# Bank sums, load queue and transposes of a streamed fp32 block: eight small changes of order in one kernel

## The chip, the cores and the metric

One Trainium2 chip, one core. The metric is the device time of one execution in microseconds (us); the time before is the median of three runs. Engines: PE is TensorE (matmuls and transposes), ACT is ScalarE, DVE is VectorE, POOL is GpSimd, SP issues the loads. Each engine works through its own list of instructions in a fixed order, and waits for the others by semaphores.

## The reference

One layer with S = 256 tokens, width D = 2048 and a hidden width FF = 5632, all in float32:

```
h = x + W_out [ DiffAttn ; ConformerConv ]( RMSNorm(x) )
hn = rms_norm(h, norm2_g)
a  = hn @ w_gate ;  bu = hn @ w_up
y  = h + (silu(a) * bu) @ w_down
```

The input projection w_in has 5120 columns; attention and convolution work on its output, and w_out (2048 x 2048) joins them. The weights are about 200 MB, each read once. The second line to the last are the feed-forward network (FFN), whose eleven blocks of 512 hidden columns take most of the time.

## The kernel before

**Products and chunks.** A float32 product is made of three products of rounded operands: hi times hi, lo times hi and hi times lo, where hi is the operand rounded to PE's fast format and lo the rest. A chunk of weights is two k-tiles (128 x 1024 elements, 512 KB). SP loads it (L300) into one of four buffers `raw`, ACT rounds it to `whi` (L305), DVE subtracts to get `wlo` (L314), and PE runs 8 matmuls with `whi` (L344, L345) and then 4 with `wlo` (L350). Matmuls are 128 x 128 by 512 columns; the two halves of the tokens (m = 0, 1) are the output rows. `run_chunks` (L372) writes out all engines' work in the order of the chunks: a chunk's load and rounding stand two or three chunks (AHEAD, HI_AHEAD) ahead of its matmuls, its subtraction two (LO_AHEAD). All other work sits in generators; `resume()` takes each running one a step on, between the halves of a chunk and at its end. So a `yield` more or less in a generator moves that step by half a chunk in every engine's list. There is no reordering after that.

**The stages.** Input projection with the convolution as side work, up to about 240 us; attention; w_out, about 260 to 350 us; block 0 of the FFN, a plain gate and up product, 350 to 420; blocks 1 to 10; and the w_down products in three groups (FGROUPS: after blocks 3, 7 and 10).

**w_out and h.** `out_done` (L726) adds a 512-column part to `h` on DVE (L729). For each of its four k-tiles PE transposes h into one PSUM bank `ps_h` (L738), ACT writes the rounded, scaled tile `hhi` from the bank (L219), DVE the rest `hlo` from the same bank (L220), and ACT reads the bank a second time for an unrounded copy `hn` (L743), which the fast blocks need. Then ACT sums squares (L405).

**make_forms** (L802) multiplies hn by the rows' factor rstd2, spread over partitions by a matmul of a matrix of ones, which POOL fills (L805), with a diagonal (L813, `ps_r`), and makes the seven sums of hn's quarters, `fhi` and `flo`, in block 0.

**Fast blocks 1 to 10.** A block is a list of twelve units. An `s` unit takes a k-tile of each half of the weights' rows, gate and up together, in seven products of sums (21 matmuls, L898 to L900), which go to seven PSUM banks; DVE makes the sums `wt` (L873 to L875) and the lower halves `wl` (L881, L882) of the weights. `g` and `u` units are plain chunks of w_gate and w_up (12 matmuls, L915, L916, L921) for the remaining k-tiles in pairs (TWOS); they use `whi` and `wlo` as above, and go on in banks Q2 and Q4 (g) or Q3 and QX (u). The order of kinds is ORDER = "sggsggsuusuu", FIRST for block 1. A block uses all eight banks, so the next block's s unit needs them back: Q3 last, for the seventh product of its first unit. `products_done` (L956) adds banks once the last s unit is through; `block_done` (L974) starts after the last unit, adds Q3 and QX (L980), multiplies with the silu (L983), and after some steps `transposed` (L782) turns the result in two sets of four transposes (L789, `ps_a`), each rounded on ACT and split on DVE (L793).

**w_down.** `down_done` (L987) adds to `h` (L995) and, in the last group, stores to the output from SP's queue (L997), in which the loads of the weights stand too. Every third chunk of w_down loads into `spare_raw`, one of two large buffers of the pool `early` (tag wb), which the s units use else.

Of the kernel before, what the change touches and what calls it, by code (L numbers as in the profile page):

```python
# [12 lines left out]
F32 = mybir.dt.float32  # L13
# [5 lines left out]
P = 128  # L19
# [51 lines left out]
NS = 4  # L71
REST = [k for k in range(KD) if k % HK >= NS]
TWOS = [tuple(REST[i : i + 2]) for i in range(0, len(REST), 2)]
BY_DMA = []

ORDER = "sggsggsuusuu"

FIRST = "guggsusgssuu"

Q1, Q6, Q7, Q5, Q2, Q4, Q3, QX = range(8)  # L80

# [16 lines left out]
def tile_block(  # L98
# [273 lines left out]
    def run_chunks():  # L372
        n = len(chunks)
        i = j = 0
        for t in range(n):
            hi_lead, lo_lead = lead(t)
            while j < min(i, t + 1 + lo_lead):
                chunks[j]["split"](chunks[j])
                j += 1
            while i < min(n, t + 1 + hi_lead):  # L380
                if i in before:
                    before[i]()
                chunks[i]["load"](chunks[i])
                chunks[i]["round"](chunks[i])
                i += 1
                if hi_lead == lo_lead:
                    chunks[j]["split"](chunks[j])
                    j += 1
            while j < min(n, t + 1 + lo_lead):
                chunks[j]["split"](chunks[j])  # L390
                j += 1
            chunks[t]["multiply"](chunks[t])
            if chunks[t].get("spare_raw") is not None and chunks[t]["done"]:
                resume()
        while running:
            resume()
# [329 lines left out]
    def out_done(n, ps):  # L726
        cs = slice(n * N, (n + 1) * N)
        for m in range(NM):
            dve.tensor_tensor(h[m][:, cs], h[m][:, cs], ps[m], ALU.add)  # L729
        if n == 2:  # L730
            held[0] -= NM
        yield
        for t in range(N // P):
            k = n * (N // P) + t
            yield from room(1)
            pt = aux_ps.tile([P, N], F32, tag="aux", name="ps_h")
            for m in range(NM):
                pe.transpose(pt[:, m * P : (m + 1) * P], h[m][:, k * P : (k + 1) * P], ident)  # L738
            hT[k] = lhs_pair("h", k)
            split_scaled(hT[k], pt[:, :S], col("g2", k))  # L740
            if k % HK == 0:
                hn.append(early.tile([P, HK, S], F32, tag="wb", name="hn"))
            act.activation(hn[k // HK][:, k % HK, :], pt[:, :S], AF.Copy, scale=col("g2", k))  # L743
            if t % 2:
                yield
        for m in range(NM):
            square_sum(h[m][:, cs], ss2[m][:, n : n + 1])
        if n == D // N - 1:
            yield
            for m in range(NM):  # L750
                ss = small.tile([P, 1], F32, tag="ssh", name="ssh")
                dve.tensor_reduce(ss, ss2[m], AX.X, ALU.add)
                rsqrt_mean(rstd2[m], ss, D, EPS)
            yield
            yield
            prestack.close()
            ffn["pool"] = ctx.enter_context(tc.tile_pool(name="ffn", bufs=1))
            start(make_forms())
# [42 lines left out]

    def make_forms():  # L802
        fp = ffn["pool"]
        ones = fp.tile([P, P], F32, tag="sum0", name="ones")
        pool.memset(ones, 1.0)  # L805
        diag = fp.tile([P, S], F32, tag="sum1", name="diag")
        for m in range(NM):
            act.activation(diag[:, m * P : (m + 1) * P], ident, AF.Copy, scale=rstd2[m])
        yield
        yield  # L810
        ps = aux_ps.tile([P, N], F32, tag="aux", name="ps_r")
        for m in range(NM):
            pe.matmul(ps[:, m * P : (m + 1) * P], ones, diag[:, m * P : (m + 1) * P], start=True, stop=True)  # L813
        yield
        rb = fp.tile([P, S], F32, tag="sum2", name="rb")
        act.copy(rb, ps[:, :S])
        yield
        for i in range(2):
            for k in range(0, HK, 4):
                t = hn[i][:, k : k + 4, :]  # L820
                dve.tensor_tensor(t, t, rb.unsqueeze(1).to_broadcast([P, 4, S]), ALU.mult)
                yield

        nr = HK - NS
        chi = fp.tile([P, 2 * nr, S], F32R, tag="chi", name="chi")
# [101 lines left out]
    def fast_block(j, order, after_down):  # L927
# [20 lines left out]
            users = [c for c in units if q in c["uses"]]  # L948
            users[0]["first"][q] = users[-1]["last"][q] = True
        [c for c in units if c["kind"] == "s"][-1]["done"] = products_done  # L950
        units[-1]["done"] = lambda sums: block_done(j, sums)
        chunks.extend(units)

    halfway = {}
# [1 line left out]
    def products_done(q):  # L956

        fp = ffn["pool"]
        w1, u2, u3, w4 = (fp.tile([P, N], F32, tag=f"sum{i}", name=f"sum{i}") for i in range(4))
        act.copy(w1, q[Q1])  # L960
        yield
        yield
        dve.tensor_tensor(u2, q[Q6], w1, ALU.add)
        dve.tensor_tensor(u3, q[Q7], u2, ALU.add)
        dve.tensor_tensor(w4, q[Q5], u3, ALU.add)
        dve.tensor_tensor(u2, q[Q5], u2, ALU.add)
        yield
        dve.tensor_tensor(w1, q[Q2], w1, ALU.add)
        dve.tensor_tensor(u3, q[Q4], u3, ALU.add)
        act.activation(w1, w1, AF.Silu)  # L970
        act.activation(u3, u3, AF.Silu)
        halfway.update(g=(w1, u3), u=(u2, w4))

    def block_done(j, q):  # L974
        while "g" not in halfway:
            yield
        g, u = halfway.pop("g"), halfway.pop("u")
        yield
        for m, i in enumerate((Q3, QX)):
            dve.tensor_tensor(u[m], q[i], u[m], ALU.add)  # L980
        yield
        for m in range(NM):
            dve.tensor_tensor(u[m], u[m], g[m], ALU.mult)  # L983
        yield from lag(3)
        yield from transposed(j, u)

    def down_done(g, n, ps):  # L987
        cs = slice(n * N, (n + 1) * N)
        parts = 2 if g == len(FGROUPS) - 1 and n == D // N - 1 else 1
        for m in range(NM):  # L990
            for i in range(parts):
# [2 lines left out]
                hs = slice(cs.start + i * w, cs.start + (i + 1) * w)  # L994
                dve.tensor_tensor(h[m][:, hs], h[m][:, hs], ps[m][:, ws], ALU.add)  # L995
                if g == len(FGROUPS) - 1:
                    sp.dma_start(out=out[m * P : (m + 1) * P, hs], in_=h[m][:, hs])  # L997
        yield


# [13 lines left out]
    for ks, first, last in ((range(0, 4), True, False), (range(4, 8), False, False), (range(8, 16), False, True)):  # L1014
        for n in range(3):
            block(w_out, n * N, ks, fm, (lambda ps, n=n: out_done(n, ps)) if last else None,
                  bkey=("o", n), first=first, last=last, spare=n == 2)
    block(w_out, 3 * N, range(16), fm, lambda ps: out_done(3, ps))
    j0 = 0
    for g, nb in enumerate(FGROUPS):  # L1020
        for j in range(j0, j0 + nb):
# [6 lines left out]
        for n in range(D // N):  # L1028
            at = len(chunks)
            block(w_down, n * N, range(j0 * 4, (j0 + nb) * 4), fa, lambda ps, g=g, n=n: down_done(g, n, ps))  # L1030
            for i, c in enumerate(chunks[at:]):
                c["spare_raw"] = i % 3 == 2
        j0 += nb

# [31 lines left out]
```

## Time and profile before

| what | value |
|---|---|
| runs of the kernel before | 1108.98, 1111.71, 1112.03 us (median 1111.71) |
| the profiled execution's own time | 1109.13 us |
| its span on the core (first to last instruction) | 1107.3 us |
| around the span | 1.83 us |
| mean of matmuls 128 x 128 by 512, start to start, when nothing waits | 0.23 us |

The profile is one execution. In a row of the timeline stand start, busy time, engine, line, operation, output and inputs, their shape, how many (x2), and in brackets the engine's idle time just before and what ended it. A row "PE q L898 <- DVE sum L980: 8.8, 7, 3.2" of the waits says that PE's line 898 waited for DVE's line 980, 8.8 us in total, 7 times, 3.2 us at most. The busy time of a matmul is from its start to its modelled end; matmuls overlap, so the distance of starts is what a matmul costs.

### The profile page before, as it was taken

The page shows a single profiled execution, that of the slowest core. Times are in us where ns is not written, and L with a number is a line of the kernel's source. Part 1 is how long each engine was busy: PE and PEld are TensorE (multiplying, and loading weights), DVE is VectorE, ACT ScalarE, POOL GpSimd, SP SyncE. Part 2 cuts the span into 40 slices and gives each one's busy share as a digit, 9 for nine tenths or more (in the row PEclk, how much of TensorE's full clock was granted, in tenths as well). Part 3 has the DMA queues.
Part 4 walks back from the last instruction along what each step waited for, and adds up shares of the span by engine and source line. Part 5 has one row for each costly group of instructions (what it writes and reads, how often), then busy time and mean ns, then how long its engine had stood idle before and what let it go on. Part 6 is the DMA issues. An engine that isn't in the chain of part 4 may idle for free.

```text
span 1107.3 us, 13190 instructions
## 1 busy us (share of the span) xinstructions
PE 1064.9 (96%) x4836; PEld 869.4 (79%) x4836; DVE 867.2 (78%) x1051; ACT 574.2 (52%) x755; POOL 43.6 (4%) x78
## 2 busy tenths in 40 slices
PE   8999999999999998799999999999999999999988
PEld 7888888877867776587888887777788888777766
DVE  4799899898745678999664599999965589998643
ACT  6544566756755555555343455555543355554332
POOL 0030111201000000000000000000000000000000
PEclk9999999999999999999999999999999999999999
DMA  8756655544544455665445765656446666545173
GB/s 238 218 182 193 196 168 172 162 158 149 176 151 172 152 175 206 207 214 167 152 170 192 247 226 161 224 182 196 151 151 214 208 224 232 179 162 185 63 246 115
DMA packets 118734, 203.02 MB, mean 183 GB/s; under 512 B 6932, under 2 KB 28878, under 8 KB 118668
## 3 DMA queue, kind: packets, MB, share of 16 engines
q1 hardware_dynamic: 118608, 202.14, 55.3%
q8 instruction: 38, 0.62, 0.2%
q14 instruction: 28, 0.23, 0.1%
q10 hardware_dynamic: 60, 0.03, 0.0%
HBM read 200.04 MB, written 2.10 MB: 183 GB/s over the span
## 4 chain that ended last, share of the span: by engine, by line
PE 50%; DVE 9%; issue 2%; DMA 2%; ACT 1%; SPq 0%; DVEq 0%; ACTq 0%
PE acc L344 7%; PE acc L345 7%; PE acc L350 7%; PE q L916 5%; PE q L915 5%; PE q L921 5%; PE q L900 4%; PE q L898 4%; PE q L899 4%; DVE wlo L314 2%; DVE wl L882 1%; DVE wt L873 1%; DVE wl L881 1%; DMA wb<-in_w_gate_dram 1%; DMA raw<-in_w_down_dram 1%
## 5 line engine op out<-in xcount | busy, mean ns | idle before, releaser
L314 DVE TENSOR_TENSOR wlo<-raw,whi 128x1024 fp32r<-128x1024 f32 (+1 forms) x297 | 359.5, 1219 | 180.1 <-ACT whi L305 179.4
L305 ACT CAST whi<-raw 128x1024 fp32r<-128x1024 f32 (+1 forms) x297 | 309.2, 1048 | 249.5 <-PE acc L345 135.1
L344 PE MATMUL acc<-whi,ahi 128*128 128x512 f32 x384 | 150.6, 392 | 4.5 <-ACT whi L305 4.5
L345 PE MATMUL acc<-whi,alo 128*128 128x512 f32 x384 | 149.7, 390 | 0.2 <-DVE alo L793 0.2
L344 PE MATMUL acc<-whi,xhi 128*128 128x512 f32 (+1 forms) x352 | 130.9, 378 | 3.7 <-ACT xhi L219 3.0
L877 ACT CAST wh<-wt 128x2048 fp32r<-128x2048 f32 x40 | 76.5, 1913 | 106.2 <-DVE wt L875 106.2
L345 PE MATMUL acc<-whi,xlo 128*128 128x512 f32 (+1 forms) x352 | 129.4, 374 | 0.4 <-DVE xlo L220 0.4
L915 PE MATMUL q<-whi,chi 128*128 128x512 f32 x320 | 127.0, 397 | 0.0
L916 PE MATMUL q<-whi,clo 128*128 128x512 f32 x320 | 126.3, 395 | 0.0
L898 PE MATMUL q<-wh,fhi 128*128 128x512 f32 x280 | 111.6, 398 | 10.0 <-DVE sum L980 8.8
L900 PE MATMUL q<-wl,fhi 128*128 128x512 f32 x280 | 110.3, 394 | 4.5 <-DVE wl L882 3.7
L899 PE MATMUL q<-wh,flo 128*128 128x512 f32 x280 | 109.1, 390 | 0.0
L481 DVE SCALAR_TENSOR_TENSOR y<-upad,cw,y 128x256 f32<-128x256 f32 x240 | 103.5, 482 | 2.4 <-ACT y L474 1.9
L350 PE MATMUL acc<-wlo,ahi 128*128 128x512 f32 x384 | 103.0, 389 | 0.0
L882 DVE TENSOR_TENSOR wl<-wt,wh 128x2048 fp32r<-128x2048 f32 x40 | 91.5, 2289 | 7.2 <-ACT wh L877 7.2
L350 PE MATMUL acc<-wlo,xhi 128*128 128x512 f32 (+1 forms) x352 | 88.2, 375 | 1.2 <-DVE wlo L314 1.2
L344 PEld LDWEIGHTS acc<-whi,ahi 128*128 128x128 f32 x384 | 72.1, 188 | 20.4 <-ACT whi L305 5.8
L921 PE MATMUL q<-wlo,chi 128*128 128x512 f32 x320 | 86.9, 393 | 0.0
L345 PEld LDWEIGHTS acc<-whi,alo 128*128 128x128 f32 x384 | 72.1, 188 | 15.7 <-DVE alo L793 1.0
L350 PEld LDWEIGHTS acc<-wlo,ahi 128*128 128x128 f32 x384 | 72.0, 188 | 15.0
L344 PEld LDWEIGHTS acc<-whi,xhi 128*128 128x128 f32 x352 | 67.3, 191 | 15.4 <-ACT xhi L219 3.4
L345 PEld LDWEIGHTS acc<-whi,xlo 128*128 128x128 f32 x352 | 67.3, 191 | 11.9 <-DVE xlo L220 0.9
(192 smaller groups left out, 1384.3 us busy)
## 6 DMA issues: line engine op xcount, KB each, us to landing
raw<-in_w_down_dram SPq DMA_DIRECT2D x88, 512.0 KB, 4.0
raw<-in_w_in_dram SPq DMA_DIRECT2D x48, 512.0 KB, 3.5
raw<-in_w_gate_dram SPq DMA_DIRECT2D x48, 512.0 KB, 4.4
raw<-in_w_up_dram SPq DMA_DIRECT2D x48, 512.0 KB, 3.7
wb<-in_w_up_dram SPq DMA_DIRECT2D x40, 512.0 KB, 3.6
wb<-in_w_gate_dram SPq DMA_DIRECT2D x40, 512.0 KB, 4.5
raw<-in_w_out_dram SPq DMA_DIRECT2D x32, 512.0 KB, 3.5
raw<-in_w_in_dram SPq DMA_DIRECT2D x62, 256.0 KB, 3.2
```

Of the source, the lines that this page charges most:

```text
L305: act.copy(c["hi"], c["raw"])
L314: dve.tensor_tensor(c["lo"], c["raw"], c["hi"].bitcast(F32), ALU.subtract)
L344: pe.matmul(ps[m], xhi[:, ms], hi[:, j, :], start=c["first"] and j == 0, stop=False)
L345: pe.matmul(ps[m], xlo[:, ms], hi[:, j, :], start=False, stop=False)
L350: pe.matmul(ps[m], xhi[:, ms], lo[:, j, :], start=False, stop=c["last"] and j == nk - 1)
L481: dve.scalar_tensor_tensor(y[:, ct, :], src, wk, y[:, ct, :], ALU.mult, ALU.add)
L898: pe.matmul(ps, fhi[:, f, p, :], c["hi"][:, w], start=bool(first), stop=False)
L899: pe.matmul(ps, flo[:, f, p, :], c["hi"][:, w], start=False, stop=False)
L900: pe.matmul(ps, fhi[:, f, p, :], c["lo"][:, w], start=False, stop=bool(last))
L915: pe.matmul(ps, x1[:, ms], hi[:, i, :], start=i == 0 and bool(c["first"].get(q)), stop=False)
L916: pe.matmul(ps, x2[:, ms], hi[:, i, :], start=False, stop=False)
L921: pe.matmul(sum_bank(c, q), forms["plain"][k][0][:, ms], lo[:, i, :], start=False, stop=i == 1 and bool(c["last"].get(q)))
```

## The change

Line numbers of the kernel after are one to seven lines off those before: `out_done` L744 to L747, products of s units L900 to L902, of g and u units L917, L918 and L923, DVE's wt L875 to L877 and wl L883, L884, the transposes L794 with their split L798, stores L998. L314, L980 and L983 are the same.

1. **By DMA.** The last residue pair of each block's g and u units (k-tiles 14 and 15) gets `wlo` in another way: ACT writes minus the rounded weights into it (L308), and a DMA issued by POOL (L309) adds `raw` to that. DVE's L314 is gone for these 20 chunks. POOL issued no DMA before.
2. **FIRST** is another order of kinds for block 1.
3. **prompt.** A block's or a w_down block's generator is stepped once more right after its last chunk; before, this was done for chunks whose key `spare_raw` was set at all.
4. **h.** `out_done` transposes two k-tiles into one bank, ACT reads the bank twice for `hn` (L744), rounds both tiles at once from `hn` in SBUF (L746), and DVE makes the rest from there (L747).
5. **make_forms** spreads the factor by an ACT write (`rep`) and two transposes, without POOL's ones, and has one step less.
6. **Bank sums.** A yield fewer or at another place in `products_done` and `block_done`; `lag(2)` for `lag(3)`.
7. **Stores** of the last w_down group go to POOL's queue, but for the last column part.
8. **Buffers.** Every third chunk of w_in and w_out, too, may load into `early`.

```diff
-BY_DMA = []
+BY_DMA = TWOS[-1:]
-FIRST = "guggsusgssuu"
+FIRST = "gugusgsgsusu"
...
-            if chunks[t].get("spare_raw") is not None and chunks[t]["done"]:
+            if chunks[t].get("prompt") and chunks[t]["done"]:
                 resume()
...
-        for t in range(N // P):
+        for t in range(0, N // P, 2):
             k = n * (N // P) + t
             yield from room(1)
-            pt = aux_ps.tile([P, N], F32, tag="aux", name="ps_h")
-            for m in range(NM):
-                pe.transpose(pt[:, m * P : (m + 1) * P], h[m][:, k * P : (k + 1) * P], ident)
-            hT[k] = lhs_pair("h", k)
-            split_scaled(hT[k], pt[:, :S], col("g2", k))
+            pt = aux_ps.tile([P, 2, S], F32, tag="aux", name="ps_h")
+            for i in range(2):
+                for m in range(NM):
+                    pe.transpose(pt[:, i, m * P : (m + 1) * P], h[m][:, (k + i) * P : (k + i + 1) * P], ident)
...
-            act.activation(hn[k // HK][:, k % HK, :], pt[:, :S], AF.Copy, scale=col("g2", k))
-            if t % 2:
-                yield
+            rows = hn[k // HK][:, k % HK : k % HK + 2, :]
+            for i in range(2):
+                act.activation(rows[:, i, :], pt[:, i, :], AF.Copy, scale=col("g2", k + i))
+            hi, lo = lhs_two("h", k)
+            act.copy(hi, rows)
+            dve.tensor_tensor(lo, rows, hi.bitcast(F32), ALU.subtract)
...
+            yield
...
-        ones = fp.tile([P, P], F32, tag="sum0", name="ones")
-        pool.memset(ones, 1.0)
-        diag = fp.tile([P, S], F32, tag="sum1", name="diag")
-        for m in range(NM):
-            act.activation(diag[:, m * P : (m + 1) * P], ident, AF.Copy, scale=rstd2[m])
-        yield
+        rep = fp.tile([P, S], F32, tag="sum1", name="rep")
+        for m in range(NM):
+            act.activation(rep[:, m * P : (m + 1) * P], ident, AF.Identity, bias=rstd2[m], scale=0.0)
...
-            pe.matmul(ps[:, m * P : (m + 1) * P], ones, diag[:, m * P : (m + 1) * P], start=True, stop=True)
+            pe.transpose(ps[:, m * P : (m + 1) * P], rep[:, m * P : (m + 1) * P], ident)
...
-        units[-1]["done"] = lambda sums: block_done(j, sums)
+        units[-1].update(done=lambda sums: block_done(j, sums), prompt=True)
...
         act.copy(w1, q[Q1])
         yield
-        yield
         dve.tensor_tensor(u2, q[Q6], w1, ALU.add)
         dve.tensor_tensor(u3, q[Q7], u2, ALU.add)
+        yield
         dve.tensor_tensor(w4, q[Q5], u3, ALU.add)
         dve.tensor_tensor(u2, q[Q5], u2, ALU.add)
-        yield
         dve.tensor_tensor(w1, q[Q2], w1, ALU.add)
+        act.activation(w1, w1, AF.Silu)
...
     def block_done(j, q):
...
         g, u = halfway.pop("g"), halfway.pop("u")
-        yield
         for m, i in enumerate((Q3, QX)):
             dve.tensor_tensor(u[m], q[i], u[m], ALU.add)
         yield
...
-        yield from lag(3)
+        yield from lag(2)
...
-                    sp.dma_start(out=out[m * P : (m + 1) * P, hs], in_=h[m][:, hs])
+                    (sp if n == D // N - 1 else pool).dma_start(out=out[m * P : (m + 1) * P, hs], in_=h[m][:, hs])
...
+    for i, c in enumerate(chunks[len(XPARTS) : -12]):
+        c["spare_raw"] = i % 3 == 2
```

The rounding and the accumulating DMA, which the kernel before has already but does not use since its BY_DMA is empty:

```
act.activation(c["lo"], c["raw"], AF.Copy, scale=-1.0)
pool.dma_start(out=c["lo"], in_=c["raw"].bitcast(F32R), accum_op=ALU.add)
```

**ACT at the first h transposes of w_out.** `hhi` and `hn` are the outputs for h (a pair of k-tiles has one `hhi`), `whi` the rounded weights, `junk` the sums of squares. Before:

```order
L305 CAST whi<-raw 128x1024 x4
L219 ACTIVATE hhi_3203<-ps_h,cols 128x256
L743 ACTIVATE hn<-ps_h,cols 128x256
L219 ACTIVATE hhi_3203<-ps_h,cols 128x256
L743 ACTIVATE hn<-ps_h,cols 128x256
L305 CAST whi<-raw 128x1024
L219 ACTIVATE hhi_3232<-ps_h,cols 128x256
L743 ACTIVATE hn<-ps_h,cols 128x256
L219 ACTIVATE hhi_3232<-ps_h,cols 128x256
L743 ACTIVATE hn<-ps_h,cols 128x256
```

And after:

```order
L305 CAST whi<-raw 128x1024 x4
L744 ACTIVATE hn<-ps_h,cols 128x256 x2
L746 CAST hhi_3208<-hn 128x512
L305 CAST whi<-raw 128x1024
L744 ACTIVATE hn<-ps_h,cols 128x256 x2
L746 CAST hhi_3233<-hn 128x512
```

Each pair of k-tiles had four ACT instructions on two banks, in turn with DVE's `hlo` from the same bank; it has three now on one bank, and none of them stands behind a DVE instruction of the pair.

**DVE from block 5 to block 6.** The L980 rows are the last bank sums of block 5 and the L983 rows its products; `wlo` and `wt` belong to the second g unit and the second s unit of block 6, `wl` to that s unit, `alo` to block 5's first transposes. Before:

```order
L314 TENSOR_TENSOR wlo<-raw,whi 128x1024
L873 TENSOR_TENSOR wt<-wb 128x1024
L874 TENSOR_TENSOR wt<-wb,wt 128x512
L875 TENSOR_TENSOR wt<-wt,wb 128x512
L980 TENSOR_TENSOR sum_6139<-q_5890,sum_6139 128x512
L980 TENSOR_TENSOR sum_6141<-q_6061,sum_6141 128x512
L983 TENSOR_TENSOR sum_6139<-sum_6139,sum_6138 128x512
L983 TENSOR_TENSOR sum_6141<-sum_6141,sum_6140 128x512
L881 TENSOR_TENSOR wl<-wb,wh 128x1536
L882 TENSOR_TENSOR wl<-wt,wh 128x2048
L314 TENSOR_TENSOR wlo<-raw,whi 128x1024
L793 TENSOR_TENSOR alo_6242<-ps_a,ahi_6241 128x512
```

And after:

```order
L980 TENSOR_TENSOR sum_6123<-q_5880,sum_6123 128x512
L980 TENSOR_TENSOR sum_6125<-q_6044,sum_6125 128x512
L314 TENSOR_TENSOR wlo<-raw,whi 128x1024
L875 TENSOR_TENSOR wt<-wb 128x1024
L876 TENSOR_TENSOR wt<-wb,wt 128x512
L877 TENSOR_TENSOR wt<-wt,wb 128x512
L983 TENSOR_TENSOR sum_6123<-sum_6123,sum_6122 128x512
L983 TENSOR_TENSOR sum_6125<-sum_6125,sum_6124 128x512
L798 TENSOR_TENSOR alo_6203<-ps_a,ahi_6202 128x512
L883 TENSOR_TENSOR wl<-wb,wh 128x1536
L884 TENSOR_TENSOR wl<-wt,wh 128x2048
L798 TENSOR_TENSOR alo_6231<-ps_a,ahi_6230 128x512
```

The sums of the banks (L980) have moved ahead of `wlo` and `wt`; the products (L983) have stayed behind them.

**PE at the same place.** q_6213 (before) and q_6205 (after) are bank Q3 of block 6, the seventh product of its first s unit; L921 and L923 with `wlo` are the end of its first g unit. Before:

```order
L900 MATMUL q_6213<-wl,fhi 128x512
L915 MATMUL q_6203<-whi,chi 128x512
L916 MATMUL q_6203<-whi,clo 128x512
L915 MATMUL q_6207<-whi,chi 128x512
L916 MATMUL q_6207<-whi,clo 128x512
L915 MATMUL q_6203<-whi,chi 128x512
L916 MATMUL q_6203<-whi,clo 128x512
L915 MATMUL q_6207<-whi,chi 128x512
L916 MATMUL q_6207<-whi,clo 128x512
L921 MATMUL q_6203<-wlo,chi 128x512 x2
L921 MATMUL q_6207<-wlo,chi 128x512 x2
L789 MATMUL ps_a<-ident,sum_6139 128x128
```

And after:

```order
L902 MATMUL q_6193<-wl,fhi 128x512
L794 MATMUL ps_a<-ident,sum_6123 128x128
L794 MATMUL ps_a<-ident,sum_6125 128x128
L794 MATMUL ps_a<-ident,sum_6123 128x128
L794 MATMUL ps_a<-ident,sum_6125 128x128
L900 MATMUL q_6205<-wh,fhi 128x512
L901 MATMUL q_6205<-wh,flo 128x512
L902 MATMUL q_6205<-wl,fhi 128x512
```

Block 5's first transposes have moved from behind the first g unit to a place inside the first s unit of block 6, ahead of its seventh product; the second set follows after the first half of the first g unit. The boundaries 2 to 3, 4 to 5, 6 to 7, 8 to 9 and 9 to 10 read alike.

**SP in the last w_down group.** `raw` are the loads of w_down, `out_dram` the stores of h. Before:

```order
L300 DMA raw<-in_w_down_dram 128x2x512 x8
L997 DMA out_dram<-h_81 128x512
L997 DMA out_dram<-h_82 128x512
L300 DMA raw<-in_w_down_dram 128x2x512 x6
L997 DMA out_dram<-h_81 128x512
L997 DMA out_dram<-h_82 128x512
```

And after:

```order
L865 DMA wb<-in_w_up_dram 128x2x512
L865 DMA wb<-in_w_gate_dram 128x2x512
L300 DMA raw<-in_w_up_dram 128x2x512 x2
L300 DMA raw<-in_w_down_dram 128x2x512 x24
L998 DMA out_dram<-h_81 128x256 x2
L998 DMA out_dram<-h_82 128x256 x2
```

All 24 loads of the group stand ahead of the only stores left in SP's queue; the other six are the last DMAs of POOL's list.

More of the change, by code (lines that the diff above doesn't have):

```diff
@@ L732, in out_done @@
         yield
-        for t in range(N // P):
+        for t in range(0, N // P, 2):
             k = n * (N // P) + t
             yield from room(1)
-            pt = aux_ps.tile([P, N], F32, tag="aux", name="ps_h")
-            for m in range(NM):
-                pe.transpose(pt[:, m * P : (m + 1) * P], h[m][:, k * P : (k + 1) * P], ident)
-            hT[k] = lhs_pair("h", k)
-            split_scaled(hT[k], pt[:, :S], col("g2", k))
+            pt = aux_ps.tile([P, 2, S], F32, tag="aux", name="ps_h")
+            for i in range(2):
+                for m in range(NM):
+                    pe.transpose(pt[:, i, m * P : (m + 1) * P], h[m][:, (k + i) * P : (k + i + 1) * P], ident)
             if k % HK == 0:
                 hn.append(early.tile([P, HK, S], F32, tag="wb", name="hn"))
-            act.activation(hn[k // HK][:, k % HK, :], pt[:, :S], AF.Copy, scale=col("g2", k))
-            if t % 2:
-                yield
+            rows = hn[k // HK][:, k % HK : k % HK + 2, :]
[4 more added lines that the diff above has]
+            dve.tensor_tensor(lo, rows, hi.bitcast(F32), ALU.subtract)
+            for i in range(2):
+                hT[k + i] = (hi[:, i, :], lo[:, i, :])
+            yield
         for m in range(NM):
@@ L961, in products_done @@
         yield
-        yield
         dve.tensor_tensor(u2, q[Q6], w1, ALU.add)
         dve.tensor_tensor(u3, q[Q7], u2, ALU.add)
+        yield
         dve.tensor_tensor(w4, q[Q5], u3, ALU.add)
         dve.tensor_tensor(u2, q[Q5], u2, ALU.add)
-        yield
         dve.tensor_tensor(w1, q[Q2], w1, ALU.add)
+        act.activation(w1, w1, AF.Silu)
         dve.tensor_tensor(u3, q[Q4], u3, ALU.add)
-        act.activation(w1, w1, AF.Silu)
         act.activation(u3, u3, AF.Silu)
@@ L1031, in tile_block @@
             for i, c in enumerate(chunks[at:]):
+                c["prompt"] = True
                 c["spare_raw"] = i % 3 == 2
```

## The prediction, made before the run

> **What bounds the kernel now.** First the page's span and its first row of engines, then what PE waits for.
>
> ```profile
> span 1107.3 us, 13190 instructions
> PE 1064.9 (96%) x4836; PEld 869.4 (79%) x4836; DVE 867.2 (78%) x1051; ACT 574.2 (52%) x755; POOL 43.6 (4%) x78
> ```
>
> PE is the bound: 1107.3 - 1064.9 = 42.4 us of its span are not matmuls, and the change leaves PE's matmuls as they are. So only PE's waits can be won or lost. The view of waits, for PE, names them:
>
> ```profile
> PE acc L344 <- ACT whi L305: 9.1, 7, 2.4
> PE q L898 <- DVE sum L980: 8.8, 7, 3.2
> PE q L900 <- DVE wl L882: 3.7, 4, 1.6
> ...
> PE ps_a L789 <- DVE alo L793: 2.7, 6, 0.5
> PE ps_h L738 <- DVE h L729: 2.7, 4, 1.1
> ...
> PE ps_h L738 <- ACT hn L743: 1.3, 2, 0.7
> PE ps_r L813 <- POOL ones L805: 1.3, 1, 1.3
> ```
>
> No row names a DMA; PE waits for ACT or DVE, seven times for the last bank sums. The same view from 300 to 405 us (w_out and block 0), then from 1050 us to the end, places the first row:
>
> ```profile
> PE acc L344 <- ACT whi L305: 3.9, 3, 2.2
> ...
> PE acc L344 <- ACT whi L305: 4.5, 3, 2.4
> ```
>
> What a wait costs is more than its idle time. PE's timeline where block 2 waits for block 1's last bank:
>
> ```profile
> 464.29 0.39 PE L899 MATMUL q<-wh,flo 128*128 128x512 f32 x1
> 464.52 0.40 PE L900 MATMUL q<-wl,fhi 128*128 128x512 f32 x1
> 468.07 0.50 PE L898 MATMUL q<-wh,fhi 128*128 128x512 f32 x1 [3.15 <-DVE sum L980]
> 468.40 0.40 PE L899 MATMUL q<-wh,flo 128*128 128x512 f32 x1
> ...
> 470.73 0.63 PE L916 MATMUL q<-whi,clo 128*128 128x512 f32 x1
> 471.16 0.63 PE L915 MATMUL q<-whi,chi 128*128 128x512 f32 x1
> ```
>
> A matmul costs 464.52 - 464.29 = 0.23. The wait makes that 468.07 - 464.52 = 3.55, and the next start 0.33 instead of 0.23: 3.32 + 0.10 = 3.42 lost where the row says 3.15. So each wait costs its idle time and 0.27. And from 469.45 on a matmul takes 0.43 (471.16 - 470.73). The view of windows shows why, and how a fast block further on stands:
>
> ```profile
> 460.00:480.00 20.00, 16.06 (x64) 12.29 (x65) 19.66 (x24) 9.69 (x10) 0.00 (x0) 0.91 0.50 161
> 682.00:726.00 44.00, 41.95 (x186) 33.85 (x185) 42.53 (x41) 24.19 (x22) 0.00 (x0) 1.00 0.59 191
> ```
>
> The columns are PE, its loads, DVE, ACT, POOL, then PE's granted clock. It was 0.91 over 20 us in the first: 1.8 us lost, the price of halving after a 3.15 us wait. In the second DVE works 42.53 of 44 us, next to PE's 41.95; what stands in DVE's list ahead of what PE needs is then time on the path.
>
> **The change part by part.** The profiled execution took 1109.13 us (span 1107.3 and 1.83 around it), 2.6 below the median of 1111.71. The sum is made against 1109.13.
>
> *h transposes (T1).* ACT, DVE and PE at the second h part:
>
> ```profile
> 323.05 0.30 PE L738 MATMUL ps_h<-ident,h 128*128 128x128 f32 x1 [1.14 <-DVE h L729]
> 323.55 0.55 PE L738 MATMUL ps_h<-ident,h 128*128 128x128 f32 x3 [0.20 <-DVE h L729]
> ...
> 324.95 0.47 ACT L743 ACTIVATE hn<-ps_h,cols 128x256 f32<-128x256 f32 x1 [0.55 <-DVE hlo L220]
> 325.32 0.47 ACT L219 ACTIVATE hhi<-ps_h,cols 128x256 fp32r<-128x256 f32 x1
> 326.34 0.47 ACT L743 ACTIVATE hn<-ps_h,cols 128x256 f32<-128x256 f32 x1 [0.55 <-DVE hlo L220]
> 326.71 1.04 ACT L305 CAST whi<-raw 128x1024 fp32r<-128x1024 f32 x1
> ```
>
> ACT and DVE take turns on a bank: 326.34 - 324.95 = 1.39 a k-tile, 0.55 of it ACT waiting for DVE, and ACT's casts of weights stand behind. Afterwards a pair is two `hn` at 0.38 apart and a cast of 512 columns, by half the 1.04 above some 0.5: 1.3 instead of 2.78, 3 us less per h part of four k-tiles. That is more than any wait that follows from it: the two for `hn`, the four for the adds (L729) that DVE reaches late behind late casts, and two of the three for casts in 300 to 405 us (3.9 - 2.2 = 1.7). 2.7 + 1.3 + 1.7 = 5.7, and 8 x 0.27 = 2.2: 7.9. PE's transposes are as many as before.
>
> *make_forms (T2, T3).* The transposes of `rep` do not wait for POOL's ones, but for rstd2, which POOL makes late: I leave 0.3 of 1.3 + 0.27, so 1.3 gained. The last wait of the stage, 2.2 + 0.27, is a cast that stands on ACT behind make_forms' steps; these come half a chunk to a chunk (1.4 to 2.75 us) earlier: 2.5 gained. T1 to T3 make 11.7; of nine waits I keep one, 0.7 on the mean: **11.0 gained**; at least 7.9.
>
> *Six block boundaries (T5).* Of 8.8 us for L980, 3.15 belong to block 1; the other six, and the six waits of `ps_a`, go: 5.65 + 2.7 + 12 x 0.27 = 11.6 removed, since sums stand first on DVE now. What comes in is read from DVE's list at such a boundary:
>
> ```profile
> 508.26 1.22 DVE L314 TENSOR_TENSOR wlo<-raw,whi 128x1024 fp32r<-128x1024 f32 x1
> 509.39 1.22 DVE L873 TENSOR_TENSOR wt<-wb 128x1024 f32<-128x1024 f32 x1
> ...
> 511.98 1.28 DVE L980 TENSOR_TENSOR sum<-q,sum 128x512 f32<-128x512 f32 x2
> 513.18 1.28 DVE L983 TENSOR_TENSOR sum<-sum,sum 128x512 f32<-128x512 f32 x2
> ```
>
> and from PE's last matmuls of the kernel, with the DVE add that follows them:
>
> ```profile
> 1102.75 0.61 PE L350 MATMUL acc<-wlo,ahi 128*128 128x512 f32 x2
> 1103.41 0.75 DVE L995 TENSOR_TENSOR h<-h,acc 128x256 f32<-128x256 f32 x2 [0.61 <-PE acc L350]
> ```
>
> DVE starts 0.05 after PE's modelled end, which is 0.21 after the next matmul could start. The new order on DVE is sums, `wlo`, `wt`, products. From PE's last matmul of the block: 0.21, L980 twice 513.18 - 511.98 = 1.20, `wlo` 1.13, `wt` 511.98 - 509.39 = 2.59, the first L983 0.68 (1.28 for two, less the 0.60 from start to start, half of 1.20): 5.81. PE reaches the first set of transposes after 18 matmuls of the next block, 18 x 0.23 = 4.13. It waits 1.68, then 0.43 for the second L983 (as at 323.55, where 0.50 stands for 0.07), and the 0.27: 2.4 a boundary, 14.3 in six. **2.7 lost**. The wait for L980 becomes one for L983, for what DVE still does in between. Behind PE's waiting transposes stand all its matmuls.
>
> *Block 1 to 2 (T4).* DVE is the bound there, so the 3.15 stays for the most part. Two `wlo` (2.3 us) leave DVE's list before the second L983, which ended at
>
> ```profile
> 468.53 1.28 DVE L983 TENSOR_TENSOR sum<-sum,sum 128x512 f32<-128x512 f32 x2
> ```
>
> 468.53 + 1.28 = 469.8, now 467.5; PE needs that one instead of L980, and goes on some 0.3 after it: 467.8 against 468.07, **0.3 gained**. The new FIRST order may win the 3.7 of `wl` L882, or lose as much again; I count nothing and keep 4 for the range.
>
> *By DMA.* Twenty `wlo` less on DVE are 20 x 1.13, but this is worth what T4 and T5 hold, no more. ACT's 20 negated copies are 2 a block, 2.1 us on 24.19 of 44. The accumulating DMA has no row in this trace. The nearest is a load of the same size:
>
> ```profile
> raw<-in_w_down_dram SPq DMA_DIRECT2D x88, 512.0 KB, 4.0
> ```
>
> Casts stand three units ahead; until PE reads `wlo` it has 12 + 21 + 12 + 8 = 53 matmuls, 12.2 us, less two ACT copies of 1.04: 10.1. The bounds for landing are 4.0 (a load) and twice that (the destination read too): 0 on the path. Past 10.1, or where POOL is held up, each us late costs PE up to 20.
>
> What POOL does while DVE runs on two SBUF inputs:
>
> ```profile
> 374.02 1.22 DVE L314 TENSOR_TENSOR wlo<-raw,whi 128x1024 fp32r<-128x1024 f32 x1
> 374.12 1.16 POOL L203 TENSOR_SCALAR rsq<-ssh 128x1 f32<-128x1 f32 x1 [86.48 <-DVE ssh L752]
> ...
> 376.01 0.19 POOL L203 TENSOR_SCALAR rsq<-ssh 128x1 f32<-128x1 f32 x1
> ```
>
> The same operation takes 1.16 and ends with DVE's, or 0.19. If issuing is held likewise, it is one DVE instruction, up to 2.3 us: still within 10.1. [...]
>
> *Stores and buffers (T6).* The last group's loads stand behind stores on SP:
>
> ```profile
> 1067.06 0.95 SPq L997 DMA_DIRECT2D out_dram<-h  x2
> 1068.10 3.83 SPq L300 DMA_DIRECT2D raw<-in_w_down_dram  x6
> ...
> 1073.54 1.04 ACT L305 CAST whi<-raw 128x1024 fp32r<-128x1024 f32 x1 [9.32 <-DMA raw<-in_w_down_dram]
> ```
>
> The stores wait for h, and loads of the next part with them; ACT idles 9.32, PE waits three times: 4.5 + 3 x 0.27 = **5.3 gained**. On POOL the stores hold nothing up, and the last are over some 12 us (one w_down part) before the end. More raw buffers: no PE wait names a load; nothing.
>
> Sum: -11.0 + 2.7 - 0.3 - 5.3 = -13.9, so 1095.2 for an execution like the profiled one. With half of the 2.6 us to the median: **1096.5**.
>
> **The rivals.**
>
> A, no new wait at the boundaries (0.08): DVE's `wt` is ready sooner than I add up, or the sums come when PE still has more ahead of it. For it: 2 `wlo` less per block on a full DVE. Against: the list is fixed, and 5.81 exceeds 4.13. Then 14.3 more: 1082.
>
> B, the clock halves at the new waits (0.15). For it: 3.15 did so, at 1.8 us. Against it stands the mean clock of the whole span:
>
> ```profile
> core 0: 1107.3 us, clock 0.997
> ```
>
> 0.003 of 1107.3 is 3.3 us: the 1.8 and a start-up leave no room for another halving, so the cast waits of 2.4 and 2.2 us did without. With 1.7 at each of six: 10 more, 1107. [...]
>
> C, half of the front's 11 and some of T6 stays (0.10): the adds come late for another reason, DVE's own `wlo` row. 1103.
>
> D, slower (0.09): the accumulating DMA lands late. Its place is the 20 units; it decides from 13.9 / 20 = 0.7 us beyond the 10.1 of cover. At 2 us late: 40 more, 1136. For it: DVE busy 42.53 of 44, POOL's 1.16 for 0.19. Against: 10.1 us are 2.5 times a load.
>
> E, no change (0.03): gains given back elsewhere on a full DVE, 1111.
>
> **How the numbers follow.** The forecast has 0.55. Its own range: 4 either way for block 1, 3 for the front, 2.6 for the run: 1090 to 1102. With B and C and the front of A: 1086 to 1108, leaving out D and most of A, some 0.17. A measurement tells some 0.3%, 3.3 us. Faster: forecast, A, C and nearly all of B, 0.86; same 0.05; slower: D, 0.09.
>
> **What would show it.** In the profile after: no waits of `ps_h`; none for L980 but block 1's; in their place six waits of `ps_a` for L983, 1.5 to 2.5 us each, with the clock at 1.00; no ACT idle for loads of w_down; no PE wait for a DMA. Wrong would be: PE waits at L923 for a DMA (D), clock under 0.95 at the boundaries (B), or L983 waits missing (A).

## The result, and the profile after

| kernel | median us (runs) | ratio to the kernel before, 95% interval |
|---|---|---|
| before | 1111.71 (1108.98 to 1112.03) | |
| after | 1097.14 (1096.67 to 1098.23) | 0.9878 [0.9851, 0.9905] |
| after, once more on another chip, where before took 1110.87 | 1096.9 | 0.9872 [0.9859, 0.9886] |

The change gains 14 us; 1096.5 was forecast. The total came out, but two of its parts did not: the experiments below show a gain of 11 us, by the DMA, where the prediction had none, and a loss of 17, by the new order, where it had 2.7.

The profiled execution after took 1098.23 us, the slowest of its three, where the one before was the fastest of its three (1109.13); so these two traces show 10.9 of the 14 us. The page's span and engines, and its row of the new DMA queue:

```profile
span 1096.4 us, 13237 instructions
...
PE 1063.8 (97%) x4834; PEld 873.6 (80%) x4834; DVE 844.6 (77%) x1023; ACT 590.3 (54%) x767; POOL 64.7 (6%) x103
...
q0 software_dynamic: 3360, 12.06, 5.9%
```

PE's matmuls are what they were; DVE lost 867.2 - 844.6 = 22.6 us, the twenty `wlo`. What PE waits for after, in the view of waits:

```profile
PE ps_a L794 <- DVE sum L983: 17.3, 19, 4.0
...
PE q L923 <- DMA wlo<-raw: 2.4, 1, 2.4
PE q L902 <- DVE wl L884: 2.0, 2, 1.2
...
PE ps_r L815 <- ACT rep L811: 0.2, 1, 0.2
```

Four things are to be seen against the rows of before. All waits for `ps_h` are gone, and those for casts (9.1 us) but for 0.2. The 8.8 us for L980 are gone, as are the 2.7 for `alo`. One row is new and larger than both: 17.3 us for the products L983, 19 times. And PE once waits for a DMA.

At a fast-block boundary (2 to 3) the new wait looks like this, on PE and then on DVE:

```profile
499.56 0.39 PE L902 MATMUL q<-wl,fhi 128*128 128x512 f32 x1
501.06 0.33 PE L794 MATMUL ps_a<-ident,sum 128*128 128x128 f32 x1 [1.12 <-DVE sum L983]
501.67 0.55 PE L794 MATMUL ps_a<-ident,sum 128*128 128x128 f32 x3 [0.28 <-DVE sum L983]
501.97 0.47 PE L900 MATMUL q<-wh,fhi 128*128 128x512 f32 x1
```

```profile
495.40 1.29 DVE L980 TENSOR_TENSOR sum<-q,sum 128x512 f32<-128x512 f32 x2 [1.05 <-PE q L923]
496.60 1.22 DVE L314 TENSOR_TENSOR wlo<-raw,whi 128x1024 fp32r<-128x1024 f32 x1
497.73 1.22 DVE L875 TENSOR_TENSOR wt<-wb 128x1024 f32<-128x1024 f32 x1
...
500.32 1.28 DVE L983 TENSOR_TENSOR sum<-sum,sum 128x512 f32<-128x512 f32 x2
```

The order is as predicted: sums, `wlo`, `wt`, products, and PE's transposes waiting for the products. DVE even stood idle for 1.05 us ahead of the sums: it had caught up with PE. PE waits 1.12 and 0.28. The same wait stands three times at the step to w_down, after blocks 3, 7 and 10, where the prediction had none. (PE has done 20 matmuls of w_down by then; below these are called the waits ahead of w_down.) The last of them on PE:

```profile
1028.51 0.33 PE L794 MATMUL ps_a<-ident,sum 128*128 128x128 f32 x1 [1.39 <-DVE sum L983]
1029.11 0.55 PE L794 MATMUL ps_a<-ident,sum 128*128 128x128 f32 x3 [0.27 <-DVE sum L983]
...
1030.42 0.62 PE L344 MATMUL acc<-whi,ahi 128*128 128x512 f32 x1
1030.85 0.63 PE L345 MATMUL acc<-whi,alo 128*128 128x512 f32 x1
```

From 1030.42 on a matmul takes 0.43 (1030.85 - 1030.42): the clock is halved behind this wait. The view of windows around it, with PE's granted clock third from the end:

```profile
1024.00:1034.00 10.00, 8.34 (x32) 6.22 (x31) 8.11 (x11) 3.70 (x5) 0.00 (x0) 0.83 0.49 163
```

At the h transposes ACT now works without a break, two `hn` and one cast a pair, no row of DVE between:

```profile
309.40 0.84 ACT L744 ACTIVATE hn<-ps_h,cols 128x256 f32<-128x256 f32 x2 [3.13 <-PE ps_h L739]
310.27 0.62 ACT L746 CAST hhi<-hn 128x512 fp32r<-128x512 f32 x1
310.79 1.04 ACT L305 CAST whi<-raw 128x1024 fp32r<-128x1024 f32 x1
```

310.79 - 309.40 = 1.39 us a pair, against 1.39 a k-tile.

### The profile page after: what moved, and what is told of

It is laid out like the page before. It is cut to its first block, busy times and chain, and to the rows that moved or that the text cites. A ratio compares the mean times of both kernels' runs of the same rounds, so it can differ in the third digit from the quotient of the medians.

```text
span 1096.4 us, 13237 instructions
## 1 busy us (share of the span) xinstructions
PE 1063.8 (97%) x4834; PEld 873.6 (80%) x4834; DVE 844.6 (77%) x1023; ACT 590.3 (54%) x767; POOL 64.7 (6%) x103
## 4 chain that ended last, share of the span: by engine, by line
PE 85%; DVE 8%; DMA 3%; issue 3%; ACT 1%; POOL 1%; SPq 0%; DVEq 0%; POOLq 0%; ACTq 0%
PE acc L350 16%; PE acc L345 16%; PE acc L344 16%; PE q L917 6%; PE q L918 6%; PE q L923 6%; PE q L900 5%; PE q L902 5%; PE q L901 5%; DVE wlo L314 2%; DVE sum L983 1%; DMA raw<-in_w_in_dram 1%; PE ps_a L794 1%; DVE sum L980 1%; DMA raw<-in_w_gate_dram 1%
## 5 line engine op out<-in xcount | busy, mean ns | idle before, releaser
L314 DVE TENSOR_TENSOR wlo<-raw,whi 128x1024 fp32r<-128x1024 f32 (+1 forms) x277 | 335.8, 1218 | 148.5 <-ACT whi L305 148.5
L917 PE MATMUL q<-whi,chi 128*128 128x512 f32 x320 | 126.6, 396 | 0.0
L918 PE MATMUL q<-whi,clo 128*128 128x512 f32 x320 | 126.2, 394 | 0.0
L902 PE MATMUL q<-wl,fhi 128*128 128x512 f32 x280 | 110.1, 393 | 2.0 <-DVE wl L884 2.0
L900 PE MATMUL q<-wh,fhi 128*128 128x512 f32 x280 | 110.7, 396 | 0.0
L884 DVE TENSOR_TENSOR wl<-wt,wh 128x2048 fp32r<-128x2048 f32 x40 | 91.6, 2290 | 8.4 <-ACT wh L879 8.1
L923 PE MATMUL q<-wlo,chi 128*128 128x512 f32 x320 | 87.3, 395 | 2.4 <-DMA wlo<-raw 2.4
```

The source lines that it names most:

```text
L314: dve.tensor_tensor(c["lo"], c["raw"], c["hi"].bitcast(F32), ALU.subtract)
L900: pe.matmul(ps, fhi[:, f, p, :], c["hi"][:, w], start=bool(first), stop=False)
L902: pe.matmul(ps, fhi[:, f, p, :], c["lo"][:, w], start=False, stop=bool(last))
L917: pe.matmul(ps, x1[:, ms], hi[:, i, :], start=i == 0 and bool(c["first"].get(q)), stop=False)
L918: pe.matmul(ps, x2[:, ms], hi[:, i, :], start=False, stop=False)
L923: pe.matmul(sum_bank(c, q), forms["plain"][k][0][:, ms], lo[:, i, :], start=False, stop=i == 1 and bool(c["last"].get(q)))
```

## The experiments

Each is timed against the kernel before on its own chip, four or more runs of each.

| what | median us | ratio, 95% interval |
|---|---|---|
| after, products behind the sums | 1094.13 | 0.9851 [0.9836, 0.9865] |
| after, no DMA for wlo | 1108.11 | 0.9976 [0.9967, 0.9985] |
| after, stores on SP | 1103.14 | 0.9935 [0.9920, 0.9949] |
| after, old h transposes | 1108.14 | 0.9974 [0.9966, 0.9983] |
| after, old steps of the sums | 1079.40 | 0.9718 [0.9704, 0.9731] |
| before, DMA alone | 1100.14 | 0.9900 [0.9887, 0.9914] |
| before, new steps alone | 1127.41 | 1.0158 [1.0144, 1.0172] |
| after, transposes two steps later | 1078.95 | 0.9719 [0.9706, 0.9732] |
| products first, transposes spread | 1076.90 | 0.9692 [0.9678, 0.9705] |
| the same, DMA from block 2 | 1078.65 | 0.9718 [0.9705, 0.9731] |
| after, old order of block 1 | 1097.01 | 0.9883 [0.9870, 0.9897] |

**After again**, beside the runs of the DMA alone, the old steps and the spread version.

> The kernel after once more, beside the three below and on their chip: 1096 to 1099 by every theory.

1096.9, as the table of the result has it.

**Products first.** The first theory was that of the prediction: the new wait is there because `wlo` and `wt` stand on DVE between sums and products. The edit takes them from between:

```diff
             dve.tensor_tensor(u[m], q[i], u[m], ALU.add)
-        yield
         for m in range(NM):
             dve.tensor_tensor(u[m], u[m], g[m], ALU.mult)
+        yield
         yield from lag(2)
```

> The kernel after, with the two products (L983) directly behind the bank sums (L980) on DVE, ahead of wlo and wt. Theory 1: the waits of ps_a for L983 are there only because wlo and wt (3.7 us) stand in between. Then the six at fast-block boundaries (1.28 + 0.53 us each) vanish, 10.9 us; the three ahead of w_down shrink from 2.08 to about 1.0, 3 us; at block 1 to 2 some 5 us go; in all 18 to 22 us less than the kernel after, 1076 to 1080. Rival: DVE is full, so the time comes back as waits for wl or wlo behind it; then 1088 to 1097 and new rows of PE waiting for wl L884 or wlo L314.

It gave 1094.13, some 3 us less than after instead of 18 to 22. From 470 us to the end PE waits for:

```profile
PE ps_a L794 <- DVE alo L798: 11.2, 6, 1.9
PE ps_a L794 <- DVE sum L982: 1.6, 6, 0.3
```

The waits for the products are nearly gone (L982 is L983 here), and six others have come, for `alo`, ahead of the second set of transposes. The rival's time came true, but not for its reason: DVE was not full. ACT and DVE at boundary 2 to 3:

```profile
500.51 1.91 ACT L879 CAST wh<-wt 128x2048 fp32r<-128x2048 f32 x1 [5.26 <-DVE wt L877]
502.32 0.58 ACT L796 CAST ahi<-ps_a 128x512 fp32r<-128x512 f32 x1
```

```profile
499.78 0.69 DVE L877 TENSOR_TENSOR wt<-wt,wb 128x512 f32<-128x512 f32 x1
502.93 0.69 DVE L798 TENSOR_TENSOR alo<-ps_a,ahi 128x512 fp32r<-128x512 f32 x1 [2.45 <-ACT ahi L796]
```

DVE idles 2.45 us for ACT's copy of the first set, which stands in ACT's list behind the cast of `wh`, which waited 5.26 for `wt`. The second set waits for this `alo`, which reads the first one's bank. So early transposes on PE are held up by either chain, and the first theory was too narrow.

**No DMA.** `BY_DMA = []` in the kernel after.

> The kernel after without the accumulating DMA: all wlo on DVE. Theory 1: the 20 wlo that the DMA takes over are worth little, since DVE waits for PE's last matmul at a block's end anyway (1.05 us idle ahead of L980): the late DMA of block 1 goes (2.7 us less), block 1 gets two wlo back (2.3 us more), some tenths at other boundaries: within 2 us of the kernel after. Rival: DVE is the bound in the fast blocks, so each wlo counts: 20 x 1.13 = 22 us more, 1119, or at least half of it.

11 us slower than after: half of the rival's 22, and far beyond 2. The same view of waits from 470 us on, in the kernel after and in this one:

```profile
PE ps_a L794 <- DVE sum L983: 13.3, 18, 1.4
```

```profile
PE ps_a L794 <- DVE sum L983: 18.7, 18, 2.6
```

5.4 us more in the same 18 waits, since a `wlo` more stands in DVE's list; and the granted clock was lower, 0.991 over the span against 0.993, which makes some 2 us (from 675 to 690 us it was 0.89 here and 1.00 in the kernel after). The theory that the DMA is worth little fell. Theory 2, formed from these two runs: the DMA gains by shortening DVE's list ahead of the sums, and the new steps lose what they gain.

**DMA alone.** `BY_DMA = TWOS[-1:]` in the kernel before, nothing else.

> The kernel before with the accumulating DMA alone. Theory 2: the six waits for L980 (0.8 to 1.7 us each with their follow-up) go or nearly so, block 1 loses two wlo from DVE's list but may wait for one late DMA; 6 to 10 us less than the kernel before. Rival, as the prediction has it: without the new order of the sums the DMA is worth nothing by itself: within 2 us of the kernel before.

10.7 us faster than before, a little more than the 6 to 10 expected. From 470 to 1035 us PE waits for:

```profile
PE ps_a L789 <- DVE alo L793: 0.5, 1, 0.5
PE acc L345 <- DVE alo L793: 0.2, 1, 0.2
```

Those were six waits for L980 and six for `alo`, 5.65 and 2.7 us. With two `wlo` a block less, DVE reaches the sums in time in the old order too. This is the gain that the prediction had booked under the new order.

**Old steps.** The kernel after with the old `products_done`, `block_done`, and no `prompt` on a block's last unit.

> The kernel after with the old steps of products_done and block_done, and without the extra step after a block's last unit: the bank sums stand behind wlo and wt again; all else is new. Theory 2 (the DMA's wlo shorten DVE's list ahead of the sums, and the new place of the transposes costs as much as it gains): the waits for L980 shrink to some tenths, those of ps_a for alo stay at 0.6 x 6, the three ahead of w_down (6.2 us) and their halving of the clock (1.7) are gone: 1082 to 1090, faster than the kernel after. Rival: the early bank sums are what makes the kernel after faster; then it is slower than the kernel after by 5 us or more.

1079.40, 17.5 us faster than the kernel after, and below the expected range. From 470 us to the end (L982 is the bank sums here):

```profile
PE q L900 <- DVE sum L982: 1.1, 1, 1.1
PE ps_a L794 <- DVE alo L798: 0.5, 1, 0.5
PE acc L345 <- DVE alo L798: 0.2, 1, 0.2
```

**New steps alone.** The kernel before with these steps and `prompt`, nothing else.

> The kernel before with the new steps of products_done and block_done and the extra step after a block's last unit, and nothing else of the change. Theory 3: the waits for L983 come in place of those for L980, longer than in the kernel after since two wlo a block are still on DVE, with three more ahead of w_down and the clock halved once or more: 8 to 20 us slower than the kernel before. Rival, as the prediction has it: a loss of 2.7 us or less, 1111 to 1114.

17.4 us slower than before, with DVE's `wlo` still all there. From 480 to 1055 us:

```profile
PE ps_a L789 <- DVE sum L981: 18.4, 17, 2.6
```

(L981 is L983 here.) Done alone or undone alone, this part of the change costs the same 17.5 us. Theory 3 says which half of it does.

**Transposes two steps later.** This asks which half of the new steps costs: that the products stand behind `wt` on DVE, or that the transposes stand early on PE. Only `lag(2)` becomes `lag(4)` in the kernel after.

> The kernel after with lag(4) for lag(2): the sums of the banks stay early, the products stay behind wlo and wt on DVE, only the transposes stand two steps later on PE, after the first half of the first g unit. Theory 3 (what costs in the new order is the place of the transposes on PE, inside the s unit, not the products' place on DVE): PE reaches the first set 6.7 us after the block's end, the second product is ready at about 5.9; no wait there; the second set waits for alo, which is behind wl now, some 0.7 + 0.27 each; ahead of w_down nothing: 1078 to 1086. Rival: the products behind wt are the cost; then 1090 to 1097.

1078.95: PE's place of the transposes is the cost. The products stay behind `wt`. From 470 us on:

```profile
PE ps_a L794 <- DVE alo L798: 2.7, 6, 0.5
```

**Spread.** Both: products first, the first set behind the s unit, the second set later.

```diff
-            yield
+            yield from lag(3 if j and t == 0 else 1)
...
-        yield
         for m in range(NM):
             dve.tensor_tensor(u[m], u[m], g[m], ALU.mult)
-        yield from lag(2)
+        yield
+        yield from lag(3)
```

> The products directly behind the bank sums, the first set of transposes one step later than in the kernel after (ahead of the first g unit, behind the s unit), and the second set two steps more. Theory 2: in the run with the products first PE waited for alo, which stands behind ACT's copy of ps_a, which stands behind the cast of wh, which waits for wt. With the sets further apart nothing on PE waits for this chain: the six boundaries cost nothing (10.9 us less than the kernel after), the three ahead of w_down nothing (6.2), block 1 to 2 some 4 less: 1074 to 1079. Rival: a full DVE gives it back as waits for wl; then 1088 or more, with rows of PE waiting for wl L883 or L884.

1076.90, as expected and the fastest of all: 20 us less than after, 34 less than before. From 470 us on one wait is left:

```profile
PE acc L345 <- DVE alo L798: 0.5, 1, 0.5
```

**The same, DMA from block 2 on.** `by_dma=what in BY_DMA and j > 1`.

> The spread version with the DMA from block 2 on only. The one wait for a DMA (3.2 us and its follow-up, 3.4, with the clock halved behind it once, 1.7) goes; block 1 gets two wlo of 1.13 back on DVE, which is the bound there. If the first outweighs: 1 to 4 us less than the spread version, 1073 to 1076; if the second: 1077 to 1080.

1078.65, 1.75 more as it stands and 0.0026 or 2.9 us by the ratios, whose intervals just touch: two `wlo` on DVE in block 1 seem to cost more than the one late DMA.

**Stores on SP.** `sp.dma_start` for all stores.

> The kernel after with all stores of the last group back on SP's queue. Theory 1: loads of the next w_down part stand behind stores that wait for h, and PE waits three times for casts as before: 5.3 us more, 1102 to 1103. Rival: the larger number of buffers or the earlier steps hide it, no change.

1103.14, by the ratios 0.0063 or 7 us more than after. From 1030 us on:

```profile
PE acc L344 <- ACT whi L305: 4.2, 3, 2.3
```

**Old h transposes.** The old `out_done` in the kernel after.

> The kernel after with out_done as before (one k-tile per bank, hhi and hlo from PSUM, hn by a second read). Theory 1: the six waits of ps_h and two for casts come back: 7 to 9 us more, 1104 to 1106. Rival: they were due to something else (buffers, the order of the loads) and stay away: no change.

11 us more than after, where 7 to 9 were expected. The eight waits are back from 300 to 405 us, and one more than expected, for `rep`:

```profile
PE ps_h L738 <- DVE h L729: 2.7, 4, 1.1
PE ps_r L810 <- ACT rep L806: 2.1, 2, 1.5
PE acc L344 <- ACT whi L305: 1.7, 2, 0.9
PE ps_h L738 <- ACT hn L743: 1.3, 2, 0.7
```

Over a slow `out_done` the transposes of the new make_forms wait 2.1 us for ACT, more than the old ones' 1.3 for POOL: T2's gain is there only with T1's. The cast wait of 2.2 us that the prediction put down to make_forms' steps (T3) stays away in this run. No run has make_forms alone taken out.

**Old order of block 1.** The old FIRST.

> The kernel after with the old order of block 1. Every theory leaves the other blocks alone. If the new order was made for the DMA (in the old order the by-DMA g unit stands earlier and waited 4.6 us with the DMA alone), one DMA wait of 2 to 5 us, with waits of wl as before: 2 to 6 us more than the kernel after. Rival, as the prediction has it: nothing, within 2 us.

1097.01, no change, as the prediction counted. One DMA wait is longer (3.6 us) and the waits of L983 at that boundary shorter.

## Why the prediction was right, and where its steps failed

**The front (T1 to T3): right.** 11.0 predicted. From 300 to 405 us PE waits 0.2 us for what it named, and block 1's first matmul starts at 399.00 us instead of 410.41, 11.4 earlier (the rows are shown below). With the old h transposes it starts at 408.25 in the trace of that run, 9.3 later than in the trace after; the median is 11 us longer. The 2.2 us that are left are about the size of T3's cast wait (2.2 + 0.27), whose cause, make_forms or the buffers, was not told apart.

**The stores (T6): right.** 5.3 predicted, 7 measured by the ratios, three casts of 4.2 us as named.

**Block boundaries (T5): the wait was there, the books were wrong.** What the prediction described is in the trace, place by place. Three sizes were off. The wait is 1.40 us (1.12 + 0.28) instead of 1.68 + 0.43, since the first sum waits only for bank Q3, whose last matmul is two ahead of the block's end: 0.46 that the sum of 5.81 had too much. The three ahead of w_down, 1.39 + 0.27 and the same follow-up, were left out: PE passes 20 matmuls there, which looked like cover enough, but DVE's chain of bank sums starts late there. Its first row at block 3's end, in the kernel after:

```profile
537.74 0.69 DVE L964 TENSOR_TENSOR sum<-q,sum 128x512 f32<-128x512 f32 x1 [6.79 <-ACT sum L962]
```

DVE idles 6.79 us for ACT's first copy of a bank (L962), then has the bank sums to do in one go. And the 11.6 us that the prediction set against the new waits were no gain of the new order. With the DMA these waits go in the old order as well (DMA alone), and the new order then costs 17.5.

**The DMA: the step that failed.** "Twenty `wlo` less on DVE are 20 x 1.13, but this is worth what T4 and T5 hold, no more." It is worth 10.7 alone and 11 on top of the rest. The prediction had seen DVE busy for 42.53 of 44 us and the L980 waits behind `wlo` and `wt`; the next step, taking the `wlo` out of that same list, was not made, because the new order had already been credited with the whole wait. Two edits against one stall were booked as one. Each was to be asked what it does without the other: the DMA shortens the list, the new order moves the need ahead of it.

So T5 and the DMA together were put at +2.7 and measure 17.5 - 10.7 = +6.8; the front and stores were put at -16.3, and undoing the h transposes and the stores measures -11 - 7 = -18. The total was right because the stall was counted once, whoever removed it; the parts were not. That it came within 1 us of 1096.5 is in part luck: a loss 4 us larger stands against a gain 2 us larger, and the two profiled executions, for which -13.9 was added up, differ by 10.9.

The parts measured singly sum to -11.2 of the 14 us. T3 is not in them, and its 2.4 us would be most of the rest. In the two traces, which show 10.9 us, one can add up by stages. PE's first matmul of block 1 and of the last w_down group, before:

```profile
410.41 0.39 PE L915 MATMUL q<-whi,chi 128*128 128x512 f32 x1
...
1030.80 0.39 PE L344 MATMUL acc<-whi,ahi 128*128 128x512 f32 x1
```

and after:

```profile
399.00 0.39 PE L917 MATMUL q<-whi,chi 128*128 128x512 f32 x1
...
1022.42 0.39 PE L344 MATMUL acc<-whi,ahi 128*128 128x512 f32 x1
```

11.4 us are gained up to block 1, 3.0 lost from there to the last w_down group (623.4 against 620.4 us, two of the three waits ahead of w_down among them), and 2.5 gained in that group, where the third of these waits costs some 3.9 (1.39 + 0.27, twice 0.27, and 1.7 for the clock); by this estimate the stores alone gain some 6.4.

**The accumulating DMA: bounds nearly right, one place missed.** Landing was put at 4 to 8 us against 10.1 of cover. The trace's issues after:

```profile
wlo<-raw POOLq DMA_DIRECT2D x20, 512.0 KB, 5.5
```

5.5 at the median, 8.5 at most; PE waited for one of twenty, in block 1, 2.4 us. The prediction worked out the cover for blocks 2 to 10 only. Block 1's has less of it: ACT's negated copy comes late there behind casts that wait for `wt`, so that PE is at its `wlo` 5.9 us after the issue (422.02 to 427.93). This DMA was also a slow one, 8.3 us: at the median of 5.5 it would have come in time.

**Rivals.** A (no new wait) did not come, though the version with the transposes spread shows that it was to be had: 1076.90. B came at none of the six boundaries (granted clock 1.00 from 470 to 1024 us); the clock was halved behind the wait ahead of the last w_down group (0.83 over 10 us, so 1.7 lost), and not by the wait's length alone, see below. C did not come: the front's and the stores' waits are gone. D did not come: no DMA was late in nine of ten blocks. E did not come either.

**Block 1 (T4).** The wait there is 4.0 us in this trace (the longest of its row), where 3.15 stood; the gain of 0.3 is not in it. It stands beside the late DMA (2.4 us) and a granted clock of 0.76 from 448 to 462 us, and with the transposes two steps later the longest wait for L983 is 1.9; its parts were not told apart.

## What to carry to other kernels

Where two edits attack one stall, work out each without the other before booking the sum; the total may be right and one of the edits still a loss. When a consumer is moved ahead on one engine (here transposes on PE), list all that stands ahead of its inputs on each engine in turn, the copy on ACT behind another cast as well as the product on DVE: freeing one of the chains only shows the next. On a nearly full engine (DVE, 42.53 of 44 us), taking instructions out of its list ahead of a barrier was worth half their time (10.7 us alone, for 22.6); moving the barrier's consumer later was worth more (1078.95 against 1097.14 us).

## What the hardware showed that was not expected

**The same wait came three times, and the clock was halved behind one.** After, PE waits 1.39 us and then 0.27 or 0.28 ahead of each group of w_down, with the first transpose at 545.74, 809.14 and 1028.51 us. The granted clock was 1.00 from 536 to 556 us and from 795 to 820, and 0.83 from 1024 to 1034 (above). Before, PE waited 2.44 us near the end, and the clock stayed at 1.00:

```profile
1074.64 0.50 PE L344 MATMUL acc<-whi,ahi 128*128 128x512 f32 x1 [2.44 <-ACT whi L305]
```

```profile
1070.00:1080.00 10.00, 7.56 (x34) 5.94 (x33) 4.90 (x4) 4.70 (x5) 0.00 (x0) 1.00 0.86 300
```

Around the longer waits at block 1's end it was lower: 0.91 from 460 to 480 us before (3.15 us of wait), 0.76 from 448 to 462 us after (3.96). So in these two traces a wait's length did not decide alone; what else did was not shown.

**POOL's issue of a DMA was not held up by DVE.** The prediction weighed that it might be. The kernel after's instructions at such an issue:

```profile
683.49 0.88 POOL L309 DMA_DIRECT2D wlo<-raw  x1 [22.93 <-DVE alo L798]
```

```profile
683.28 1.22 DVE L314 TENSOR_TENSOR wlo<-raw,whi 128x1024 fp32r<-128x1024 f32 x1
684.41 1.22 DVE L875 TENSOR_TENSOR wt<-wb 128x1024 f32<-128x1024 f32 x1
```

0.88 us, while DVE ran on two SBUF inputs without a break. All 20 issues took 0.87 to 1.08: the eight that fell wholly inside one L314 row 0.87 to 0.90, and the three during which DVE was idle 0.88 to 0.90 as well. In the trace of before, POOL's L203, which reads, took 1.16 beside DVE's L314, and 0.19 at its next turn.

**An accumulating DMA from SBUF to SBUF** of 512 KB landed in 4.5 to 8.5 us, 5.5 at the median, where the groups of 512 KB loads took 3.5 to 5.5 at the median in the same run; with the DMA alone one took 10.5.
